# Split token rows of an input projection begin at four places modulo 256 bytes, and eight idle matmuls stand at the beginning in place of fourteen

## The chip, the cores and the metric

The kernel runs on one core of a Trainium2 chip. The metric is the device time of one execution in microseconds, lower is better. Engines are named as in the profile: PE is TensorE (PEld its weight loads), DVE is VectorE, ACT is ScalarE, POOL is GpSimd, SP is SyncE, which issues most of the DMAs.

## The reference

One layer of a hybrid decoder for 4096 prompt tokens and 64 sample tokens (8 sequences of 8), model width 1024. In short:

```python
h = _rmsnorm(x, g_pre)
z = h @ w_in                      # 1024 -> 2816 columns
cb, cc, ch, cg, q, k, v, ag, mq, mg = _split_cols(z)
u = cc * ch                       # gated short convolution
out_a = silu(cg) * cb * conv3(u)
out_b = silu(ag) * window_attention(q, k, v, sink)   # window of 128
out_c = silu(mg) * memory_attention(mq, mk, mv)      # 256 memory tokens
y = concatenate([out_a, out_b, out_c]) @ w_out
x = x + _rmsnorm(y, g_post)
```

All arrays are float32.

## The kernel before, in words

The work falls into two parts. The first, up to about 930 us, is the input projection `h @ w_in`. The second is attention and the output projection. The change touches the first alone.

**Tiles of the projection.** The 4160 tokens are cut into 8 blocks of 520 (`NBLK`), and each block into two halves of 260 (`HW`). The 22 column tiles of `w_in` are worked off in three phases (`PHASES`) as pairs, called quads `q` in the loops: four in the first two phases, three in the last. For each block and pair the product of a 2x2 matrix of weights with a 2x2 matrix of tokens is formed by seven products (`PRODUCTS`, a Strassen-Winograd scheme: A and S are weights or sums of them, B and T are tokens or sums of them). The first two blocks of the first phase are the exception: they take eight plain products (`plain_block`).

**Split numbers.** Each operand is split in two float32r parts, `hi` (the rounded copy, by ACT) and `lo` (the rest, by DVE), so that three matmuls make one product of full accuracy: w_hi x hi, w_hi x lo, w_lo x hi. `product` (L363, its matmul at L368) does this for 4 slices `k` of the contraction, 12 matmuls a call, each of 128 weights by 260 columns and each with a weight load of its own. The moving operand is a row of 260 numbers of a split token tile, the stationary operand a slice of a weight tile `w`.

**Where the operands lie.** Split token tiles come from the pool `hp`, two buffers for tag `hi` and two for `lo`. They are written in `split` (L355) for the seven-product blocks and in `x_split` (L577) for the plain ones. A tile holds 4 rows of `XR` = 320 numbers (1280 bytes, five times 256), of which the first 260 are used. The pool's address in a partition is a multiple of 256, and so are the tiles' sizes; therefore each of the rows begins at 0 modulo 256 bytes. The weight tiles of quads 0, 1 and 2 come from the pool `wa`, whose slices all begin at 0 modulo 256; those of quad 3 come from the pool `wb`, at the other end of the memory, whose slices begin at 224 modulo 256. In the profile a weight tile is named w_0, w_1, w_2 or w_3 by its quad, with a letter A or S; token tiles are named hi_3T, lo_3T and so on.

**The attention's operands**, which the prediction compares with: the scores of the window (L1248) take queries `q` as weights and keys `kst` as moving rows of 256 numbers. Odd chunks of 256 tokens hold both in the pool `pre`, where they begin at 160 modulo 256; even chunks from the second on hold them in `bq` and `keys`, where they begin at 0. The output projection (L1494) has moving rows of 512 numbers at 0 and weights at 0.

**Order.** The first phase's order on all engines is written out by hand (`manual_schedule`, L692). Ahead of the first product, PE runs matmuls on a tile `warm` of ones whose result nobody reads (L700 to L704); they need nothing but a memset of POOL. Meanwhile ACT and DVE split the first weights (`w_split`, L181) and tokens (`x_split`) as their DMAs land.

Of the kernel before, what the change touches and what calls it, by code (L numbers as in the profile page):

```python
# [9 lines left out]
F32R = mybir.dt.float32r  # L10
# [5 lines left out]
P = 128  # L16
D = 1024
KT = D // P
KH = KT // 2
# [4 lines left out]
HW = 260  # L24
XR = 320
# [22 lines left out]
def f(ap):  # L48
    return ap.bitcast(F32)
# [3 lines left out]
def hybrid_layer(ctx: ExitStack, tc: tile.TileContext, a: dict):  # L53
# [39 lines left out]
    hp = pa.enter_context(tc.tile_pool(name="hp", bufs=2))  # L93
# [68 lines left out]
    def store(dst, src):  # L162
        if store_queue[0] is G:
            G.dma_start(dst, src)
        else:
            late.append(lambda: DMA.dma_start(dst, src))
# [153 lines left out]
    def gain_of(o, k):  # L320
        kk = KH * (int(o[1]) - 1) + k
        return gpre[:, kk : kk + 1]
# [16 lines left out]
    def t_sum(ph, b, o):  # L339
# [9 lines left out]
        if ph == 1:  # L349
# [2 lines left out]
                tc.keep_in_program_order(ins)  # L352
            store(hd[b][o], ops[o])

    def split(src, name):  # L355
        hi = hp.tile([P, KH, XR], F32R, tag="hi", name=f"hi{name}")[:, :, :HW]
        lo = hp.tile([P, KH, XR], F32R, tag="lo", name=f"lo{name}")[:, :, :HW]
        S.copy(hi, src)
        V.tensor_tensor(lo, src, f(hi), op=ALU.subtract)
        return hi, lo  # L360
# [157 lines left out]
    def h_split(i):  # L518
        if i < len(steps):
            ph, b, p = steps[i]  # L520
            o = PRODUCTS[p][1]
            hs[i] = split(xs[ph, b][o], f"{ph}_{b}{o}")
# [52 lines left out]
    raw0, zz, pending, h0, kept = {}, {}, {}, {}, {}  # L575

    def x_split(b, o, meanwhile=lambda: None):  # L577
        x = xs[0, b][o]
        h0[b, o] = hi, lo = [hp.tile([P, KH, XR], F32R, tag=n, name=f"{n}0_{b}{o}")[:, :, :HW] for n in ("hi", "lo")]
        for k in range(KH):  # L580
            if k == 1:
                meanwhile()
            g = gain_of(o, k)
            S.mul(hi[:, k], x[:, k], g)
            V.scalar_tensor_tensor(lo[:, k], x[:, k], g, f(hi[:, k]), op0=ALU.mult, op1=ALU.subtract)
# [37 lines left out]
    def plain_jobs(b, s):  # L623

        gains = lambda b, *os: [lambda o=o: x_gain(0, b, o) for o in os]
        scales = lambda b, *os: [lambda o=o: x_scale(0, b, o) for o in os]
        parts = lambda b, o: [lambda: x_split(b, o)]
        fill = lambda o: [lambda q=q: first_fill(o, q) for q in range(4)]
        sums = lambda q, k: [lambda: first_sums(q, k)]
# [70 lines left out]
    idle = accumulator(1, 2, "idle")  # L700
    warm = hp.tile([P, KH, XR], F32R, tag="lo", name="warm").rearrange("p k n -> p (k n)")
    G.memset(f(warm[:, : P + 512]), 1.0)
    for n in (416, 416, 416, 416, 512, 512, 512, 416, 416, 416, 260, 260, 260, 260):
        TE.matmul(idle[:, 0, :n], warm[:, :P], warm[:, P : P + n], start=True, stop=True)  # L704
    x_split(0, "B11", lambda: first_fill("A21", 0))
    for q in range(4):
        if q > 0:
# [743 lines left out]
    class Block:  # L1451
# [10 lines left out]
        def split(self):  # L1462
# [13 lines left out]
            self.hl = [hi, lo]  # L1476

        def run(self, last, start, split, starts):
            b, m = self.b, self.m
            yn = work([P, D], "yn", f"yn{b}")  # L1480
# [4 lines left out]
            for p, (c0, c1) in enumerate(parts):  # L1485
                if p == 1:
                    split()
                acc = psum("z", f"y{b}_{p}")[:, : c1 - c0]
                j, passes = 0, 3 if m == P else 2
                for k in range(KT):  # L1490
                    if k in starts:
                        start()
                    for l, r in ((0, 0), (1, 0), (0, 1)) if m == P else ((0, 0), (0, 1)):
                        TE.matmul(acc, self.hl[l][:, k], wo[k][c0 // 512][:, r, c0 % 512 : c0 % 512 + c1 - c0], start=j == 0, stop=j == passes * KT - 1)  # L1494
                        j += 1
                if m < P:
                    S.copy(yn[:m, c0:c1], acc[m : 2 * m])
                    V.tensor_tensor(acc[:m], acc[:m], yn[:m, c0:c1], op=ALU.add)
                end = last and p == 2
                if not end:  # L1500
                    V.tensor_tensor(yn[:m, c0:c1], acc[:m], gpost[:m, c0:c1], op=ALU.mult)  # L1501
                S.activation((psum("t", "sq") if end else acc)[:m, : c1 - c0], acc[:m], AF.Square, scale=float(D) ** -0.5, accum_out=st[:m, p : p + 1])  # L1502
                if last and p == 1:
                    V.tensor_tensor(st[:m, 0:1], st[:m, 0:1], st[:m, 1:2], op=ALU.add)
# [180 lines left out]
```

## Time and profile before

| what | value |
|---|---|
| median of 3 runs | 1533.97 us (1533.04 to 1534.76) |
| profiled execution, its own time | 1536.78 us |
| its span, first to last instruction | 1535.0 us |
| PE busy | 1522.3 us, 99% of the span |
| DVE, ACT, POOL busy | 1145.1, 806.1, 379.7 us |
| mean granted TensorE clock | 0.999 |
| L368 (`product`): first and last start | 6.8 and about 930 us |

How to read it: the span counts from the first instruction. A row of the timeline has the start in us, the length in us, the engine, the line, the operation and its tiles (out<-in), the shape and the number of instructions merged. Consecutive matmuls overlap in it, because each one's length goes from its start to the end of its passage through the array; the rate at which PE works is the distance between starts. In the list of waits a row has who waited, for whom, the total in us, how many times and the longest.

### The profile page before, as it was taken

How to read it: one execution, taken by the hardware profiler on the slowest of the kernel's cores; microseconds unless marked ns; L12 is line 12 of the kernel's file. 1: busy time of each engine (PE TensorE's matmuls, PEld its weight loads, DVE VectorE, ACT ScalarE, POOL GpSimd, SP SyncE). 2: the span in 40 equal slices, each digit the busy share in tenths (PEclk: the TensorE clock that was granted, in tenths of full speed). 3: DMA queues.
4: the chain of work that ended last, by engine and by line, in shares of the span. 5: the costliest groups of instructions: out<-in, count | busy, mean ns of one | idle time of the engine just before them, and what ended most of it. 6: DMA issues, size and time to landing. Idle time of an engine off the chain costs nothing.

```text
span 1535.0 us, 30162 instructions
## 1 busy us (share of the span) xinstructions
PE 1522.3 (99%) x11337; PEld 1400.1 (91%) x11337; DVE 1145.1 (75%) x2055; ACT 806.1 (53%) x2039; POOL 379.7 (25%) x604
## 2 busy tenths in 40 slices
PE   9999999999999999999999999999999999999998
PEld 9999999999999999999999998788888888888777
DVE  6779888899887777897787678766666666666743
ACT  6776566476222222354454447755666556565632
POOL 0223332221300000000101203544444444444310
PEclk9999999999999999999999999999999999999999
DMA  9989999778755333678877788976776676776332
GB/s 263 194 223 242 267 288 269 280 239 286 193 181 180 126 126 126 217 227 284 237 262 230 228 298 257 237 151 160 148 148 148 151 162 149 160 159 148 130 110 96
DMA packets 177942, 306.28 MB, mean 200 GB/s; under 512 B 33925, under 2 KB 107653, under 8 KB 177765
## 3 DMA queue, kind: packets, MB, share of 16 engines
q1 hardware_dynamic: 130901, 227.38, 47.9%
q0 software_dynamic: 46176, 75.92, 24.1%
q8 instruction: 90, 1.47, 0.4%
q10 hardware_dynamic: 720, 1.05, 0.2%
q14 instruction: 55, 0.45, 0.1%
HBM read 197.23 MB, written 108.05 MB: 199 GB/s over the span
## 4 chain that ended last, share of the span: by engine, by line
PE 92%; DVE 4%; ACT 1%; DMA 1%; issue 1%; POOL 0%; SPq 0%; ACTq 0%; DVEq 0%; POOLq 0%
PE c L368 53%; PE y L1494 23%; PE ws L1248 4%; PE wo L1090 2%; PE wt L1271 2%; PE xs L1184 2%; PE xt L1199 2%; PE wo L1220 2%; PE wo L1226 1%; PE mem_acc L791 1%; DMA ws20A<-in_w_in 0%; DMA wr_1A<-in_w_in 0%; DMA ws18A<-in_w_in 0%; DVE x_2T L348 0%; DVE z L375 0%
## 5 line engine op out<-in xcount | busy, mean ns | idle before, releaser
L1494 PE MATMUL y<-wo,mh 128*128 128x512 f32 (+1 forms) x1040 | 350.5, 400 | 0.0
L375 DVE TENSOR_TENSOR z<-c,z 128x520 f32<-128x520 f32 (+1 forms) x308 | 194.2, 644 | 86.6 <-PE c L368 85.2
L1494 PEld LDWEIGHTS y<-wo,mh 128*128 128x128 f32 x1040 | 194.3, 188 | 39.2 <-issue 2.4
L1494 PE MATMUL y<-wo,ml 128*128 128x512 f32 (+1 forms) x520 | 201.8, 388 | 0.0
L1261 ACT ACTIVATE sm<-sm,wnm 128x128 f32<-128x128 f32 x256 | 99.6, 391 | 60.3 <-DVE wnm L1255 59.5
L1193 POOL TENSOR_SCALAR xp<-xp,xrd 128x256 f32<-128x256 f32 x128 | 74.6, 589 | 207.9 <-DVE xrd L1189 207.9
L1494 PEld LDWEIGHTS y<-wo,ml 128*128 128x128 f32 x520 | 98.2, 189 | 16.4
L1185 DVE TENSOR_REDUCE xmx<-xs 128x2 f32<-128x512 f32 x64 | 44.0, 688 | 60.0 <-PE xs L1184 59.9
L1273 ACT COPY wpt<-wt 128x512 f32<-128x512 f32 x64 | 37.2, 582 | 88.5 <-PE wt L1271 85.9
L1248 PEld LDWEIGHTS ws<-kst,q 128*128 128x128 f32 x512 | 69.7, 189 | 5.6 <-ACT xp L1188 0.7
L1501 DVE TENSOR_TENSOR yn<-y,gpost 128x512 f32<-128x512 f32 (+1 forms) x66 | 45.0, 681 | 39.9 <-PE y L1494 39.6
L1248 PE MATMUL ws<-kst,q 128*128 128x256 f32 x512 | 73.0, 283 | 0.4 <-ACT xp L1188 0.4
L1502 ACT ACTIVATE y<-y 128x512 f32<-128x512 f32 (+1 forms) x66 | 38.6, 585 | 64.0 <-DVE yn L1501 64.0
L739 POOL CAST wmask<-negs 128x256 uint8<-128x256 f32 x1 | 0.9, 877 | 267.9 <-DMA negs<-in_wmask 267.9
L1281 POOL TENSOR_SCALAR_AFFINE_SELECT wpt<-wpt 128x512 f32<-128x512 f32 x64 | 52.6, 822 | 42.2 <-ACT wpt L1273 39.3
L1188 ACT ACTIVATE xp<-xs,xnm 128x256 f32<-128x256 f32 x128 | 58.9, 464 | 7.1 <-DVE xnm L1186 7.1
L1123 POOL DMA_DIRECT2D q<-qd x64 | 42.8, 673 | 70.4 <-DMA qd<-zh 60.5
L1112 POOL DMA_DIRECT2D kst<-qd x64 | 38.6, 617 | 63.8 <-PE xt L1199 41.6
L1512 DVE SCALAR_TENSOR_TENSOR xr<-yn,yst,xr 128x1024 f32<-128x1024 f32 (+2 forms) x34 | 43.1, 1269 | 15.1 <-POOL yst L1508 13.2
L1251 DVE COPY_PREDICATED sm<-wmask,ws 128x256 f32<-128x256 uint8 x124 | 52.1, 436 | 2.4 <-ACT sm L1250 2.0
L1278 POOL TENSOR_SCALAR_AFFINE_SELECT wpv<-wpt 128x512 f32<-128x512 f32 x62 | 41.1, 662 | 50.8 <-ACT wpt L1273 50.8
L276 ACT ACTIVATE nat<-nat 104x1024 f32<-104x1024 f32 x40 | 42.2, 1056 | 19.2 <-DMA nat<-in_x_p 19.2
(962 smaller groups left out, 5096.8 us busy)
## 6 DMA issues: line engine op xcount, KB each, us to landing
q<-qd POOLq DMA_DIRECT2D x64, 384.0 KB
xr<-in_x_p SPq DMA_DIRECT2D x32, 512.0 KB
nat<-in_x_p SPq DMA_DIRECT2D x39, 416.0 KB
o_yp<-xr SPq DMA_DIRECT2D x31, 512.0 KB
md<-th POOLq DMA_DIRECT2D x48, 260.0 KB
qd<-zh SPq DMA_DIRECT2D x48, 260.0 KB
qd<-z SPq DMA_DIRECT2D x48, 260.0 KB
kst<-qd POOLq DMA_DIRECT2D x60, 192.0 KB
```

The source lines that it names most:

```text
L368: TE.matmul(bank[:, :HW], l, r, start=first and i == 0, stop=last and i == 3 * KH - 1)
L375: add = lambda dst, other: V.tensor_tensor(dst, c, other, op=ALU.add)
L1185: V.tensor_reduce(mx[:, :nb], s, axis=AX.X, op=ALU.max)
L1188: S.activation(p[:, i, :], s[:, i, :], AF.Exp, bias=nm[:, i : i + 1], scale=SCALE, accum_out=den[:, i : i + 1])
L1193: G.tensor_scalar(p[:, i, :], p[:, i, :], rd[:, i : i + 1], 0.5, op0=ALU.mult, op1=ALU.mult)
L1248: TE.matmul(s3[:, hh, :], self.q[:, 4 + 2 * (2 * half + hh) + kvh, i * P : i * P + P], self.kst[:, 2 * kvh + part, i * P : i * P + 2 * P], ...
L1251: V.copy_predicated(sm[:, 2 * half : 2 * half + 2, :], third["wmask"], third["negs"] if first else s3[:, :, 0:P])
L1261: S.activation(sm[:, hh, :], sm[:, hh, :], AF.Exp, bias=nm[:, hh : hh + 1], scale=SCALE, accum_out=den[:, hh : hh + 1])
L1281: G.affine_select(p3, p3, pattern=[[0, 4], [1, P]], compare_op=ALU.is_ge, fill=0.0, base=0, channel_multiplier=-1)
L1494: TE.matmul(acc, self.hl[l][:, k], wo[k][c0 // 512][:, r, c0 % 512 : c0 % 512 + c1 - c0], start=j == 0, stop=j == passes * KT - 1)
L1501: V.tensor_tensor(yn[:m, c0:c1], acc[:m], gpost[:m, c0:c1], op=ALU.mult)
L1512: V.scalar_tensor_tensor(self.xr[:m, cs], yn[:m, cs], st[:m, 3:4], self.xr[:m, cs], op0=ALU.mult, op1=ALU.add)
```

## The change

A helper `split_tile` hands out the split tiles in both places. It uses the same tiles of 4 x 320 numbers, but a row's 260 numbers now begin at number 8 or 16 of the 320 for `hi`, and at 40 or 48 for `lo`, in turn from one tile to the next. In bytes modulo 256 that is 32 or 64 for `hi` and 160 or 192 for `lo`. Since each tag has two buffers that are used in turn as well, each buffer has one place for good, and a step's `hi` and `lo` are always 32 and 160, or 64 and 192. The tile `warm` is not affected. Separately, the list of idle matmuls is cut after its eighth.

```diff
+    begins = {"hi": [8, 16], "lo": [40, 48]}
+
+    def split_tile(tag, name):
+
+        n = begins[tag][0]
+        begins[tag].reverse()
+        return hp.tile([P, KH, XR], F32R, tag=tag, name=name)[:, :, n : n + HW]
+
     def split(src, name):
-        hi = hp.tile([P, KH, XR], F32R, tag="hi", name=f"hi{name}")[:, :, :HW]
-        lo = hp.tile([P, KH, XR], F32R, tag="lo", name=f"lo{name}")[:, :, :HW]
+        hi, lo = split_tile("hi", f"hi{name}"), split_tile("lo", f"lo{name}")
         S.copy(hi, src)
         V.tensor_tensor(lo, src, f(hi), op=ALU.subtract)
...
     def x_split(b, o, meanwhile=lambda: None):
         x = xs[0, b][o]
-        h0[b, o] = hi, lo = [hp.tile([P, KH, XR], F32R, tag=n, name=f"{n}0_{b}{o}")[:, :, :HW] for n in ("hi", "lo")]
+        h0[b, o] = hi, lo = [split_tile(n, f"{n}0_{b}{o}") for n in ("hi", "lo")]
...
-    for n in (416, 416, 416, 416, 512, 512, 512, 416, 416, 416, 260, 260, 260, 260):
+    for n in (416, 416, 416, 416, 512, 512, 512, 416):
```

No instruction changes its place otherwise. The only difference in the order is at the beginning of PE, before the first product's 12 matmuls (idle and warm are the idle matmuls' accumulator and operand, c the first accumulator). Before:

```order
L704 MATMUL idle<-warm 128x416 x4
L704 MATMUL idle<-warm 128x512 x3
L704 MATMUL idle<-warm 128x416 x3
L704 MATMUL idle<-warm 128x260 x4
L368 MATMUL c_0_0_0_274<-hi_0B_236,w_0A_240 128x260
```

And with the change:

```order
L711 MATMUL idle<-warm 128x416 x4
L711 MATMUL idle<-warm 128x512 x3
L711 MATMUL idle<-warm 128x416
L375 MATMUL c_0_0_0_268<-hi_0B_230,w_0A_234 128x260
L375 MATMUL c_0_0_0_268<-lo_0B_231,w_0A_234 128x260
```

Two idle matmuls of 416 columns and four of 260 are gone; the products follow in the same order as before, with their lines seven higher.

## The prediction

> **What bounds the kernel now.** I read the page's busy table first, then the chain of work that ended last, then the waits of TensorE, and last the timeline of TensorE in single products.
>
> ```profile
> span 1535.0 us, 30162 instructions
> PE 1522.3 (99%) x11337; PEld 1400.1 (91%) x11337; DVE 1145.1 (75%) x2055; ACT 806.1 (53%) x2039; POOL 379.7 (25%) x604
> PE 92%; DVE 4%; ACT 1%; DMA 1%; issue 1%; POOL 0%; SPq 0%; ACTq 0%; DVEq 0%; POOLq 0%
> PE c L368 53%; PE y L1494 23%; PE ws L1248 4%; PE wo L1090 2%; PE wt L1271 2%; PE xs L1184 2%; PE xt L1199 2%; PE wo L1220 2%; PE wo L1226 1%; PE mem_acc L791 1%; DMA ws20A<-in_w_in 0%; DMA wr_1A<-in_w_in 0%; DMA ws18A<-in_w_in 0%; DVE x_2T L348 0%; DVE z L375 0%
> ```
>
> TensorE is busy for 99% of the span and holds 92% of the chain, and 53% of the chain is one line, L368: the matmuls of `product`, whose moving rows are the tiles that the change shifts. There is no wait worth removing in front of them:
>
> ```profile
> PE idle L704 <- POOL warm L702: 2.2, 1, 2.2
> PE wt L1271 <- DVE xrd L1189: 1.4, 1, 1.4
> PE c L368 <- DVE lo_3T L359: 0.9, 1, 0.9
> ```
>
> The largest wait of an L368 group is 0.9 us. So L368 costs what its matmuls cost back to back, and the question is how far apart their starts lie. The durations of the groups (282 ns) overlap and can't be added. The distance from one start to the next can. Here is one step, four products of 12 matmuls with the same split rows, each row being a product's first matmul (the column is the start):
>
> ```profile
> 152.41 0.28 PE L368 MATMUL c<-hi_3T,w_0S 128*128 128x260 f32 x1
> ...
> 153.83 0.28 PE L368 MATMUL c<-hi_3T,w_1S 128*128 128x260 f32 x1
> ...
> 155.25 0.28 PE L368 MATMUL c<-hi_3T,w_2S 128*128 128x260 f32 x1
> ...
> 156.68 0.28 PE L368 MATMUL c<-hi_3T,w_3S 128*128 128x260 f32 x1
> ...
> 158.12 0.28 PE L368 MATMUL c<-hi_3T,w_0S 128*128 128x260 f32 x1
> ```
>
> The products take 1.42, 1.42, 1.43 and 1.44 us, so 118.3 to 120 ns a matmul. The first three read weights that begin at 0 modulo 256; the fourth, w_3, reads weights that begin at 224 (pool `wb`). Its moving rows are the same ones. Places matter here, then, but by about 1.4 ns in 119.
>
> **The split rows.** The program has 7,488 matmuls at L368 (8 plain steps for 2 blocks, 7 products for 6 blocks, 7 for 8 blocks, all of 4 quads, and 7 for 8 blocks of 3 quads, each 12 matmuls). No instruction is added, and ScalarE and VectorE write the same shapes to other columns of the same tiles. Each nanosecond of distance is therefore 7.5 us, all of it on the path, since TensorE waits for nobody. What the new places do to the distance is not in the trace: all rows begin at 0 now. The nearest rows are the attention scores, with 256 columns, where two sets of buffers alternate. In the first group below keys and queries both begin at 160 modulo 256, in the second both at 0:
>
> ```profile
> 1007.76 1.11 PE L1248 MATMUL ws<-kst,q 128*128 128x256 f32 x8
> 1008.71 0.60 PE L1199 MATMUL xt<-ident,xp 128*128 128x128 f32 x4
> ```
>
> ```profile
> 1020.73 0.39 PE L1494 MATMUL y<-wo,ml 128*128 128x512 f32 x1
> ...
> 1021.87 1.11 PE L1248 MATMUL ws<-kst,q 128*128 128x256 f32 x8
> 1022.83 0.60 PE L1199 MATMUL xt<-ident,xp 128*128 128x128 f32 x4
> ```
>
> Eight matmuls up to the next group's start take 0.95 us at 160 and 0.96 us at 0: 118.75 against 120 ns, 1.25 ns less away from 0. The starts are rounded to 0.01 us, so this is 0 to 2.5 ns.
>
> The bounds. On the side of a loss: the fourth product's 1.44 us against a mean of 1.423 for the other three, 1.4 ns, on the 6,120 matmuls whose weights begin at 0 (all but w_3's 114 products of 12): +8.6 us. On the side of a gain: the five 512-column matmuls from 1020.73 to 1021.87 are 228 ns apart, the 256-column ones 120, so 256 more columns cost 108 ns, 0.42 ns a column, and 260 columns cost 110 ns with nothing else in them. That would take 9 ns from each and 67 us from the whole; it is the floor, not a likely value.
>
> The row on the gain's side at 160 is the nearest: `lo` now begins at 160 or 192, and all split rows leave 0. I take it: 1.25 ns x 7,488 = **-9.4 us**. The case against it is that there the weights moved along, and here they stay at 0 or 224.
>
> The Trainium skill speaks against any effect: in "TensorE: Matmul & The Clock Gate", Part 2, the rows that stream and the next weights are read through two independent ports, so that loading the one takes nothing from the other, and "SBUF — State Buffer", section Operand start alignment, states its rule for legality and timed nothing. By that the sum would be 0 us here. The trace disagrees by the 1.44 against 1.42 us above. The first page's matmul gap, 2.5 ns over the pure column time, would be 110.8 ns for 260 columns; it agrees with the floor worked out from rows.
>
> **The idle matmuls.** Six go: two of 416 columns and four of 260.
>
> ```profile
> 2.16 4.82 PE L704 MATMUL idle<-warm 128*128 128x416 f32 x14 [2.16 <-POOL warm L702]
> 6.82 0.28 PE L368 MATMUL c<-hi_0B,w_0A 128*128 128x260 f32 x1
> 6.93 0.28 PE L368 MATMUL c<-lo_0B,w_0A 128*128 128x260 f32 x1
> ...
> 8.84 0.39 PE L368 MATMUL c<-hi_0B,w_1A 128*128 128x260 f32 x1 [0.21 <-DVE w_1A L186]
> ```
>
> ```profile
> 5.01 0.60 ACT L182 CAST w_0A<-wr_0A 128x512 fp32r<-128x512 f32 x1
> 7.44 0.62 ACT L182 CAST w_1A<-wr_1A 128x512 fp32r<-128x512 f32 x1 [0.60 <-DMA wr_1A<-in_w_in]
> 8.09 0.69 DVE L186 TENSOR_TENSOR w_1A<-wr_1A,w_1A 128x512 fp32r<-128x512 f32 x1 [0.55 <-ACT w_1A L182]
> ```
>
> The fourteen stream 5,488 columns in 4.82 us, 0.88 ns a column: half the pace of the rows from 6.82 on, which are 0.11 to 0.12 us apart. Eight stream 3,616 columns and end near 2.16 + 3.2 = 5.3 us. The first product can then begin once w_0A is cast, at 5.6 us, instead of 6.8. It gains nothing: the third matmul of the second product still waits for w_1A, which VectorE hands over at 8.8 us, because its load lands at 7.4. Everything before 8.84 is slack. The cover is gone only if TensorE is still at half pace at 8.84. Full pace came 4.6 us after the first idle matmul; if those 4.6 us counted anew from 5.6, full pace would come at 10.2, and 1.4 us at half pace lose 0.7 us. I take 0, with +0.7 as the end.
>
> The Trainium skill ("TensorE: Matmul & The Clock Gate", Part 1) puts the change of pace at the end of a busy window of about 3.4 us whose phase is free; by an estimate from it, a window missed would cost about half of it, 1.7 us. The trace's 4.6 us fits a window and part of one before it.
>
> **The sum.** The profiled execution took 1536.78 us (its span 1535.0), 2.81 above the median of 1533.97. 1536.78 - 9.4 = 1527.4, and on the median's level **1524.6 us**.
>
> **The rivals.**
>
> *A, slower: what counts is the distance between rows and weights.* Then rows and weights at the same place are the good case and the change leaves it: with weights at 0, rows at 32, 64, 160, 192 are as far off as w_3's are now. The fourth product's row is the evidence for it, since only the weights' place differs there; against it, the wb tiles lie elsewhere in memory in other ways too. Price: 6,120 x 1.4 ns = 8.6 us, 1542.6 us; with a late full pace 1543. It decides as soon as a product with w_0 takes 1.44 us or more.
>
> *B, no difference.* Some of the four places save a nanosecond and some cost one, or the next matmul is held by the end of its weight load, whatever the rows do; PEld is 91% busy. Within 3 us: 1534. This is also what the skill's two ports would give.
>
> *C, much faster.* If the 9 ns above the floor are conflicts between the two reads and the new places avoid half of them, 4.5 x 7,488 = 34 us go: 1500. Against it: the rows above, with three combinations of places, all stay within 118 to 120 ns.
>
> That the rows would not move is no rival: in the program as built the 7,488 matmuls begin at 32, 64, 160 and 192.
>
> **How the numbers follow.** A change under 0.2% (3 us) can't be told from none. The forecast, a gain of 3 to 20 us, has 0.36; C, everything beyond that, 0.12; B 0.2; A 0.32. Faster 0.48, same 0.2, slower 0.32. The forecast alone lies in 1514 to 1531. The range takes in A's 1542.6 with its late pace and a rounding of 1 us, and on the other side C up to its 1500 us. Cases of both signs are in it, so it is wide. What is left out is the deeper half of C and an A worse than w_3 shows, 0.12 together.
>
> **What would show each step.** Right: the products of w_0 to w_2 near 1.41 us and w_3's no longer than 1.43; the page's L368 share falls; L1494 and the attention rows stay. A would be products of 1.44 us throughout; C products below 1.38. At the beginning the first L368 row should start near 5.7 us and the row with the wait for w_1A stay at 8.84; if that row comes later, or the products after it are 0.22 us a matmul, the trimmed idle matmuls cost time. The prediction is wrong if the distance does not change, or changes the other way, or if TensorE begins to wait for `hi` or `lo`.

## The result

| | before | changed |
|---|---|---|
| median of 5 runs, side by side | 1534.04 us (1533.04 to 1534.76) | 1540.01 us (1538.99 to 1543.66) |
| profiled execution: its own time, span | 1536.78, 1535.0 us | 1543.23, 1541.5 us |

The ratio is 1.0046, with a 95% interval from 1.0031 to 1.0061: the change makes the kernel slower by 6 us. The forecast was 1524.6 us; rival A said 1542.6.

The same lines of the changed kernel's page: span, busy times, and the chain that ended last by engine and by line. L375 is the old L368, L1501 the old L1494; all lines below `split` stand seven higher.

```profile
span 1541.5 us, 30150 instructions
PE 1529.6 (99%) x11331; PEld 1407.2 (91%) x11331; DVE 1147.0 (74%) x2055; ACT 806.8 (52%) x2039; POOL 380.8 (25%) x604
PE 93%; DVE 3%; DMA 2%; issue 1%; ACT 0%; POOL 0%; DVEq 0%; SPq 0%; POOLq 0%; ACTq 0%
```

PE's busy time grew by 7.3 us, that of its weight loads (PEld) by 7.1, the span by 6.5; the other engines moved by 2 us or less. The waits of PE (who, for whom: total us, times, longest) did not grow into anything of that size:

```profile
PE idle L711 <- POOL warm L709: 2.2, 1, 2.2
PE wt L1278 <- DVE xrd L1196: 1.7, 1, 1.7
PE c L375 <- ACT w_0A L182: 0.5, 1, 0.5
```

So the matmuls themselves stand further apart. Here are two steps of the changed kernel, eight products, from the same place as the step of before that the prediction shows (first matmul of each product; first column the start):

```profile
154.04 0.28 PE L375 MATMUL c<-hi_3T,w_0S 128*128 128x260 f32 x1
...
155.48 0.28 PE L375 MATMUL c<-hi_3T,w_1S 128*128 128x260 f32 x1
...
156.92 0.28 PE L375 MATMUL c<-hi_3T,w_2S 128*128 128x260 f32 x1
...
158.36 0.28 PE L375 MATMUL c<-hi_3T,w_3S 128*128 128x260 f32 x1
...
159.81 0.28 PE L375 MATMUL c<-hi_3T,w_0S 128*128 128x260 f32 x1
...
161.26 0.28 PE L375 MATMUL c<-hi_3T,w_1S 128*128 128x260 f32 x1
...
162.70 0.28 PE L375 MATMUL c<-hi_3T,w_2S 128*128 128x260 f32 x1
...
164.13 0.28 PE L375 MATMUL c<-hi_3T,w_3S 128*128 128x260 f32 x1
...
165.55 0.28 PE L375 MATMUL c<-hi_3T,w_0S 128*128 128x260 f32 x1
```

The first step has rows at 64 and 192: 1.44, 1.44, 1.44 and, with w_3, 1.45 us. The second has them at 32 and 160: 1.45, 1.44, 1.44 and, with w_3, 1.42 us. Before it was 1.42, 1.42, 1.43 and 1.44. Products with weights at 0 lost their 1.42 us, and w_3's lost or won by the place of the rows.

Over the whole projection, each product from the ninth on (from its first matmul to the next product's first) set against the same product of before:

| rows of hi / lo, weights at | products | change of each | together |
|---|---|---|---|
| 32 / 160, 0 | 221 | +16.8 ns | +3.7 us |
| 64 / 192, 0 | 228 | +11.7 ns | +2.7 us |
| 32 / 160, 224 | 54 | -27.8 ns | -1.5 us |
| 64 / 192, 224 | 56 | +8.1 ns | +0.5 us |
| over 1.475 us in either kernel (a wait in them) | 56 | | -1.5 us |

That is +3.8 us. The start of the projection adds 0.8 (below): the last L375 matmul starts at 934.69 us against 930.06, +4.6. The other 1.9 us of the two spans lie behind the projection, in a stretch that this execution had and the one of before had not (windows in us; the third column from the right is the granted TensorE clock):

```profile
960.00:965.70 5.70, 3.83 (x26) 3.14 (x25) 4.84 (x11) 2.73 (x8) 2.81 (x5) 1.00 1.31 273
965.70:969.10 3.40, 3.40 (x15) 3.22 (x16) 2.79 (x8) 2.21 (x10) 3.39 (x7) 0.50 1.21 272
969.10:975.00 5.90, 5.90 (x41) 3.67 (x41) 3.65 (x14) 4.59 (x20) 1.02 (x2) 1.00 1.50 291
```

For 3.4 us the clock is 0.50, by estimate 1.7 us of lost work. Two of the five runs of the changed kernel, 1543.23 and 1543.66 us, have a mean clock of 0.998 and are the slow end of its spread; the other three lie at 1538.99 to 1540.01 us.

The beginning, from the first idle matmul to the third product:

```profile
2.16 3.38 PE L711 MATMUL idle<-warm 128*128 128x416 f32 x8 [2.16 <-POOL warm L709]
6.06 0.58 PE L375 MATMUL c<-hi_0B,w_0A 128*128 128x260 f32 x1 [0.52 <-ACT w_0A L182]
6.44 0.42 PE L375 MATMUL c<-lo_0B,w_0A 128*128 128x260 f32 x1
...
9.12 0.42 PE L375 MATMUL c<-hi_0B,w_1A 128*128 128x260 f32 x1
9.34 0.42 PE L375 MATMUL c<-lo_0B,w_1A 128*128 128x260 f32 x1
...
10.84 0.28 PE L375 MATMUL c<-hi_0B,w_1A 128*128 128x260 f32 x1
10.96 0.28 PE L375 MATMUL c<-hi_0B,w_2A 128*128 128x260 f32 x1
```

The first product starts 0.8 us sooner than before (6.06 against 6.82), but its matmuls are 0.22 us apart until 9.98, where before they were 0.12 apart from the first on. The second product starts at 9.12 in place of 8.24, and the third at 10.96 in place of 10.15: 0.8 us late, and the ninth product is still as late (19.55 against 18.74).

### The profile page after: what moved, and what is told of

It reads as the page before. It is cut to its first block, busy times and chain, and to the rows that moved or that the text cites. A ratio compares the mean times of both kernels' runs of the same rounds, so it can differ in the third digit from the quotient of the medians.

```text
span 1541.5 us, 30150 instructions
## 1 busy us (share of the span) xinstructions
PE 1529.6 (99%) x11331; PEld 1407.2 (91%) x11331; DVE 1147.0 (74%) x2055; ACT 806.8 (52%) x2039; POOL 380.8 (25%) x604
## 4 chain that ended last, share of the span: by engine, by line
PE 93%; DVE 3%; DMA 2%; issue 1%; ACT 0%; POOL 0%; DVEq 0%; SPq 0%; POOLq 0%; ACTq 0%
PE c L375 55%; PE y L1501 22%; PE ws L1255 4%; PE wo L1097 2%; PE wt L1278 2%; PE xs L1191 2%; PE xt L1206 2%; PE wo L1227 2%; PE wo L1233 1%; PE mem_acc L798 1%; DMA qd<-z 1%; DVE z L382 0%; DMA wr_1A<-in_w_in 0%; DMA xr<-in_x_p 0%; DVE wo L186 0%
## 5 line engine op out<-in xcount | busy, mean ns | idle before, releaser
L1501 PE MATMUL y<-wo,mh 128*128 128x512 f32 (+1 forms) x1040 | 350.8, 400 | 0.0
L1501 PEld LDWEIGHTS y<-wo,mh 128*128 128x128 f32 x1040 | 194.5, 188 | 39.3 <-issue 2.4
L1501 PE MATMUL y<-wo,ml 128*128 128x512 f32 (+1 forms) x520 | 201.8, 388 | 0.0
L1501 PEld LDWEIGHTS y<-wo,ml 128*128 128x128 f32 x520 | 98.2, 189 | 16.5
L384 ACT COPY z<-c 128x520 f32<-128x520 f32 (+1 forms) x44 | 24.4, 554 | 52.9 <-PE c L375 50.0
```

## The experiments

Two theories stood at first. The theory of distance (rival A): the start of a moving row relative to the start of the weights, modulo 256 bytes, sets the spacing of the matmuls. Its rival: the loss comes from the shorter list of idle matmuls, or from the rows' own places whatever the weights do. Unless a diff shows otherwise, the kernels have fourteen idle matmuls. Times of products below are from start to start, means over all products of one kind shorter than 1.475 us.

**The two parts apart.** The changed kernel with the old list of idle matmuls:

```diff
-    for n in (416, 416, 416, 416, 512, 512, 512, 416):
+    for n in (416, 416, 416, 416, 512, 512, 512, 416, 416, 416, 260, 260, 260, 260):
```

> The new places with the fourteen idle matmuls kept. Theory 1 (the loss is mostly the rows' places, by their distance from the weights): the start loss of 0.8 us goes, the products of w_0 to w_2 stay at 1.436 to 1.444 us, so 1539 us, 5 us above the kernel before. Rival (the loss is mostly the late full pace, and later clock dips): 1535 us.

And the kernel before with the short list:

```diff
-    for n in (416, 416, 416, 416, 512, 512, 512, 416, 416, 416, 260, 260, 260, 260):
+    for n in (416, 416, 416, 416, 512, 512, 512, 416):
```

> The rows at 0 as before, with eight idle matmuls. Theory 1: only the start is later, by 0.8 us, so 1534.8 us, which can hardly be told from no change; products at 1.42 and 1.44 us as before; full pace first at about 10 us. Rival (idle matmuls carry the loss): 1538 to 1540 us.

The places alone: 1540.38 us, ratio 1.0043 [1.0029, 1.0057]. The idle matmuls alone: 1535.42 us, ratio 1.0007 [0.9998, 1.0016], which neither shows a loss of 0.8 us nor excludes it. The loss is nearly all the places'. The profile of the second kernel shows why its start cost next to nothing that time:

```profile
2.16 3.24 PE L704 MATMUL idle<-warm 128*128 128x416 f32 x8 [2.16 <-POOL warm L702]
5.69 0.39 PE L368 MATMUL c<-hi_0B,w_0A 128*128 128x260 f32 x1 [0.29 <-ACT w_0A L182]
5.92 0.28 PE L368 MATMUL c<-lo_0B,w_0A 128*128 128x260 f32 x1
```

Here the eight take 3.24 us and not 3.38: the trace's record of the granted clock begins with full speed at 5.10 us in this execution, before the last of them ended at 5.40, against 9.98 us in the changed kernel's. Apart from its waits the first product runs at 0.12 us a matmul. The third product starts at 10.43 us, 0.3 late.

**A map of distances.** In the changed kernel the places now rotate over eight, 32 bytes apart, from step to step, with hi and lo at the same place:

```diff
-    begins = {"hi": [8, 16], "lo": [40, 48]}
+    begins = {"hi": [0, 8, 16, 24, 32, 40, 48, 56], "lo": [0, 8, 16, 24, 32, 40, 48, 56]}
...
-        begins[tag].reverse()
+        begins[tag].append(begins[tag].pop(0))
```

> hi and lo begin at the same place, which moves by 32 bytes from one step to the next through all eight places modulo 256; fourteen idle matmuls. Each place meets weights at 0 and at 224. Theory 1 (only the distance of row and weights counts): a product with weights at 224 and rows at r takes what one with weights at 0 and rows at r+32 takes; 1.424 us at distance 0 and 1.441 at 32, so w_3 with rows at 224 takes 1.424. Theory 2 (the row's own place counts): the times go by r, the same for both weights, apart from a constant. The whole: 1534 to 1541 us.

One execution: 1542.02 us. This is the step before, the whole and the beginning of the step after the one with rows at 0 (first matmul of each product; the w_2 and w_3 rows at the top belong to rows at 224):

```profile
191.10 0.28 PE L375 MATMUL c<-hi_4B,w_2A 128*128 128x260 f32 x1
...
192.54 0.28 PE L375 MATMUL c<-hi_4B,w_3A 128*128 128x260 f32 x1
...
193.97 0.28 PE L375 MATMUL c<-hi_4T,w_0S 128*128 128x260 f32 x1
...
195.39 0.28 PE L375 MATMUL c<-hi_4T,w_1S 128*128 128x260 f32 x1
...
196.82 0.28 PE L375 MATMUL c<-hi_4T,w_2S 128*128 128x260 f32 x1
...
198.24 0.28 PE L375 MATMUL c<-hi_4T,w_3S 128*128 128x260 f32 x1
...
199.68 0.28 PE L375 MATMUL c<-hi_4T,w_0S 128*128 128x260 f32 x1
...
201.13 0.28 PE L375 MATMUL c<-hi_4T,w_1S 128*128 128x260 f32 x1
```

With rows at 224, w_2 (at 0) takes 1.44 us and w_3 (at 224) 1.43; with rows at 0, w_0 to w_2 take 1.42 to 1.43 and w_3 1.44; with rows at 32, w_0 takes 1.45. Over the kernel, distance 0 gives 1.424 us with weights at 0 and 1.425 with weights at 224, and each of the other seven distances gives 1.436 to 1.452. So distance 0 is good at either place of the weights, as the theory of distance says. Its stronger form, that the same distance always takes the same time, fails: at distance 128 the products take 1.452 us with weights at 0 and 1.438 with weights at 224, and at the other six distances the two differ by 0.5 to 6.2 ns.

Then the same with lo at 128 bytes, and at 64 bytes, behind hi:

```diff
-    begins = {"hi": [8, 16], "lo": [40, 48]}
+    begins = {"hi": [0, 8, 16, 24, 32, 40, 48, 56], "lo": [32, 40, 48, 56, 0, 8, 16, 24]}
```

> As the map with equal places, but lo begins 128 bytes from hi. Theory 1a (the distance modulo 128 counts): every product takes what the map with equal places gives for the same hi. Theory 1b (modulo 256, each matmul by its own distance): products differ between the maps, and hi at 32 with lo at 160 gives 1.441 us against weights at 0 and 1.414 against 224, as in the changed kernel. The whole: 1534 to 1541 us.

```diff
-    begins = {"hi": [8, 16], "lo": [40, 48]}
+    begins = {"hi": [0, 8, 16, 24, 32, 40, 48, 56], "lo": [16, 24, 32, 40, 48, 56, 0, 8]}
```

> The map again with lo 64 bytes from hi; fourteen idle matmuls. Theory 1 says nothing of unequal distances beyond this: where hi is at distance 0 and lo at 64, two of three matmuls stand well, so about 1.43 us; the rest 1.436 to 1.46. Rival (only hi and lo apart cost, not the weights): all products near one another. The whole 1540 to 1545 us.

One execution each: 1543.39 and 1541.07 us. That a further 128 bytes for lo would change nothing (theory 1a) failed; theory 1b holds for the pair that it named (1.441 and 1.414 us). Most pairs of distances give 1.43 to 1.46 us. Two beat even distance 0: hi at 64 and lo at 192 from the weights, 1.414 us with weights at 224 (with weights at 0, after a step at 32 and 160, 1.435), and hi at 0 and lo at 64, 1.415 us with weights at 0 and 1.416 at 224, where about 1.43 was expected. So there is something better than what the kernel before had, and lo's distance counts beside hi's.

Last, finer steps of 16 bytes with hi and lo alike:

```diff
-    begins = {"hi": [8, 16], "lo": [40, 48]}
+    begins = {"hi": [0, 4, 8, ..., 60], "lo": [0, 4, 8, ..., 60]}
```

> The map with hi and lo at the same place in steps of 16 bytes, sixteen places; fourteen idle matmuls. Theory 1: distance 0 alone gives 1.424 us, against weights at 0 and at 224 alike; 16 and 240 bytes off already cost 1.436 or more. If the good place is broad, 16 and 240 give 1.42 to 1.43. The whole 1541 to 1543 us.

One execution, 1539.14 us. That only distance 0 would do failed: with weights at 0, distances 16, 80, 144 and 240 give 1.420 to 1.425 us too, 48 gives 1.430, distance 112 the longest, 1.460, and the rest (176, 208 and every multiple of 32 but 0) 1.439 to 1.452. With weights at 224 some of these differ: 16 gives 1.434 and 80 gives 1.438. No simple rule in the distance fits this list.

**Distance 0 everywhere.** The tile `gpre` lies in front of the weights' pool. Half as large, it moves the weights of quads 0 to 2 and the rows by 32 bytes, from 0 to 224, where w_3's are already. The base is the kernel before:

```diff
-    gpre = const.tile([P, 2 * KT], F32, name="gpre")[:, :KT]
+    gpre = const.tile([P, KT], F32, name="gpre")
```

> The kernel before, with 32 bytes less ahead of the weights' first pool, so that the weights of quads 0 to 2 and all split rows begin at 224 modulo 256, where the weights of quad 3 begin already; fourteen idle matmuls. Every row then stands at distance 0 from its weights. Theory 1 (distance): all products 1.424 us; those of w_3 lose 17 ns each, 112 of them 1.9 us, so 1532.4 us. Theory 2 (a place of its own is good or bad): w_0 to w_2 change from 1.424 us and the whole moves by several us.

1533.92 us, ratio 0.9998 [0.9987, 1.0008]. In its profile the last L368 matmul starts 2.7 us earlier (927.32 against 930.06), but over the runs no difference can be told. Its products take 1.422 to 1.427 us for the most part (454 of 568 shorter than 1.475 us), but 67 take 1.440, and 27 of these follow one another:

```profile
437.51 0.28 PE L368 MATMUL c<-hi_2T,w_0S 128*128 128x260 f32 x1
...
439.33 0.28 PE L368 MATMUL c<-hi_2T,w_1S 128*128 128x260 f32 x1
...
440.77 0.28 PE L368 MATMUL c<-hi_2T,w_2S 128*128 128x260 f32 x1
...
478.21 0.28 PE L368 MATMUL c<-hi_3T,w_0S 128*128 128x260 f32 x1
...
479.76 0.28 PE L368 MATMUL c<-hi_3T,w_1S 128*128 128x260 f32 x1
...
481.19 0.28 PE L368 MATMUL c<-hi_3T,w_2S 128*128 128x260 f32 x1
```

The product from 437.51 has a wait of 0.3 us for `lo` in it (1.82 us). From 439.33 to 478.21 all 27 products take 1.440 us, then one takes 1.55, and from there on they take 1.42 again. All these rows and weights begin at 224. The places, then, do not fix the time alone: the same ones can run at two paces, and PE can change from one to the other where it waits.

**The good pair made constant.** On that base (all weights at 224) and with the helper `split_tile`, one place for all steps: hi 64 and lo 192 bytes from the weights.

```diff
+    begins = {"hi": [16], "lo": [48]}
```

> As the kernel with all operands at 224, but every hi row 64 and every lo row 192 bytes from its weights, the combination that w_3 has with half of the tiles in the changed kernel (1.414 us a product) and that w_0 to w_2 have with the other half (1.414 to 1.444). If 1.414 is what this distance gives when nothing else disturbs it: 624 products x 10 ns less than 1.424, so 1526 to 1528 us. If a product keeps the rhythm in which it began: most stay at 1.436 to 1.444, so 1539 to 1542 us.

1527.67 us, ratio 0.9946 [0.9932, 0.996]: faster than both kernels. The products, through a change of step:

```profile
155.59 0.28 PE L375 MATMUL c<-hi_3T,w_3S 128*128 128x260 f32 x1
...
157.00 0.28 PE L375 MATMUL c<-hi_3T,w_0S 128*128 128x260 f32 x1
...
158.41 0.28 PE L375 MATMUL c<-hi_3T,w_1S 128*128 128x260 f32 x1
```

Each takes 1.41 us; of 566 products shorter than 1.475 us, 540 take 1.413 or 1.414, and 16 take 1.440 or 1.441, in pairs right behind a product that waited. Its control is the same kernel with every row 32 bytes earlier, at 32 and 160 from the weights:

```diff
-    begins = {"hi": [16], "lo": [48]}
+    begins = {"hi": [8], "lo": [40]}
```

> All weights begin at 224, hi at distance 32 and lo at distance 160 from them in every step; against the kernel with distances 64 and 192 every row only begins 32 bytes earlier. If the distance sets the time: 1.44 us a product and about 1540 to 1542 us, as the changed kernel. If the distance does not matter and the constant places made the kernel at 64/192 fast: 1.414 us and about 1528 us.

1542.93 us, ratio 1.0051 [1.0036, 1.0066]: slower than the kernel before, by about as much as the changed kernel. Nearly all its products (552 of 567) take 1.44 us, and none less than 1.439, though it waits as often:

```profile
151.94 0.28 PE L375 MATMUL c<-hi_3B,w_3A 128*128 128x260 f32 x1
...
153.38 0.28 PE L375 MATMUL c<-hi_3T,w_0S 128*128 128x260 f32 x1
...
154.82 0.28 PE L375 MATMUL c<-hi_3T,w_1S 128*128 128x260 f32 x1
```

Between these two kernels nothing differs but 32 bytes in the start of the rows, and 15 us. They were timed apart, but the kernel before, timed beside each, differed by 0.9 us only (1535.05 and 1534.20), and in the two profiles the last L375 matmul starts at 922.17 and 935.38 us, so the difference arises in the projection. And the second good pair, hi at 0 and lo at 64:

```diff
-    begins = {"hi": [16], "lo": [48]}
+    begins = {"hi": [0], "lo": [16]}
```

> All weights begin at 224, hi at distance 0 from them and lo at distance 64, in every step, fourteen idle matmuls. If the pair of distances of hi and lo sets the time: products of 1.413 us as the pair 0/64 showed where eight places rotated, and about 1528 us in all. If what was seen there came from the rotation (the step before), about 1.424 to 1.44 us and 1534 to 1541 us.

1527.97 us, ratio 0.9958 [0.9943, 0.9973], products of 1.413 us: the pair is good outside the rotation too.

**Why 64 / 192 did not help the changed kernel.** It has rows at 64 and 192 with weights at 0 in every second step, a good pair by the above, yet these products take 1.436 us in the mean: 193 of 229 take 1.435 to 1.444, 28 take 1.413 to 1.416, 24 of the latter in the last phase, where PE often waits. The changed kernel with that pair in all steps (weights as they were):

```diff
-    begins = {"hi": [8, 16], "lo": [40, 48]}
+    begins = {"hi": [16], "lo": [48]}
```

> The changed kernel with one pair of places for all steps, 64 for hi and 192 for lo, in place of two pairs in turn; weights as there, at 0 for w_0 to w_2 and 224 for w_3; fourteen idle matmuls. If the changed kernel's products at 64/192 are 1.436 us because each step comes after one at 32/160: w_0 to w_2 at 1.414 us, w_3 near 1.45, about 1531 us. If it is the weights' place 0 as against 224 that spoils them: 1.436 to 1.44 us and about 1540 us.

1530.85 us, ratio 0.9978 [0.9968, 0.9988].

```profile
152.93 0.28 PE L375 MATMUL c<-hi_3T,w_1S 128*128 128x260 f32 x1
...
154.34 0.28 PE L375 MATMUL c<-hi_3T,w_2S 128*128 128x260 f32 x1
...
155.75 0.28 PE L375 MATMUL c<-hi_3T,w_3S 128*128 128x260 f32 x1
...
157.20 0.28 PE L375 MATMUL c<-hi_3T,w_0S 128*128 128x260 f32 x1
...
158.61 0.28 PE L375 MATMUL c<-hi_3T,w_1S 128*128 128x260 f32 x1
```

With weights at 0 the pair gives 1.414 us now; only w_3's, 96 and 224 bytes from its weights, is longer, 1.443 us in the mean. So it was the alternation that spoiled the pair, not the weights' place. How a step at 32 and 160 reaches into the next step is open. That it leaves the next step at the slower of two paces would fit the products at one place that took 1.440 us above, but w_3's products take 1.414 us in the middle of products of 1.44, so it is not simply that a slow product makes the next one slow.

**Eight idle matmuls on the fast kernel.**

```diff
-    for n in (416, 416, 416, 416, 512, 512, 512, 416, 416, 416, 260, 260, 260, 260):
+    for n in (416, 416, 416, 416, 512, 512, 512, 416):
```

> The kernel with distances 64 and 192 from weights at 224, now with eight idle matmuls. If the number of idle matmuls only shifts the phase in which full pace comes: within 1 us of the same kernel with fourteen, 1527 to 1529 us. If eight lose what the changed kernel's profile lost at the beginning every time: 0.8 us more.

1529.65 us, ratio 0.9968 [0.9956, 0.9981], 2.0 us above the kernel with fourteen. The two were timed apart and their intervals touch (0.9956 to 0.996), so a cost of the short list is likely here and not shown. Its profile shows the changed kernel's start again, and longer:

```profile
2.16 3.38 PE L711 MATMUL idle<-warm 128*128 128x416 f32 x8 [2.16 <-POOL warm L709]
6.41 0.58 PE L375 MATMUL c<-hi_0B,w_0A 128*128 128x260 f32 x1 [0.87 <-ACT w_0A L182]
...
11.20 0.58 PE L375 MATMUL c<-hi_0B,w_1A 128*128 128x260 f32 x2
11.62 0.28 PE L375 MATMUL c<-lo_0B,w_1A 128*128 128x260 f32 x1
...
11.87 0.28 PE L375 MATMUL c<-hi_0B,w_2A 128*128 128x260 f32 x1
```

Nearly all of the first two products run at 0.22 us a matmul, and the third starts at 11.87. In the eleven profiles with fourteen idle matmuls it starts between 9.87 and 10.81, and at most six of the first thirty distances are near 0.22 us; with eight it starts at 10.43, 10.96 and 11.87, with five, thirteen and nineteen of them.

## Why the prediction was wrong

**What bounds the kernel: right.** The time is the spacing of L368's matmuls. Without any new wait, a shift of the rows by 32 bytes moved the whole kernel by up to 15 us (1527.67 against 1542.93), in the mean 2.0 ns for each of 7,488 matmuls.

**The split rows: wrong in sign, and this is the step that failed.** The prediction took -1.25 ns a matmul from the attention scores (0.95 us for eight at 160, 0.96 at 0) as "the nearest" row, because the new places too were away from 0. It named the flaw itself: "there the weights moved along". In those rows keys and queries begin at the same place in both groups, distance 0 both times, so they could say nothing of a distance, and the difference shown was within the rounding of the starts (over all such groups of the trace, in whole ns, it is about 0.4 ns a matmul). What the change varies is the distance, and with weights at 0 it cost 1.4 ns a matmul at 32 and 160 (16.8 ns in 12) and 1.0 at 64 and 192 (11.7 ns), where a gain of 1.25 was forecast. The row that did vary the distance was the fourth product's, and it was used as a bound. That its 1.4 ns hit the size is in part luck: its rows stand at 32 for `hi` and `lo` alike, a pair that the changed kernel does not have.

**Rival A: right that the rows' start against the weights' counts, and nearly right in size,** with a chance of 0.32 where 0.48 went to a gain. Its premise that equal starts are the good case and all others cost alike is wrong: 64 and 192, or 0 and 64, are better than equal starts where they are constant, and the 2.7 us at 64 and 192 come from the alternation, which A does not have. So the nearness of its sum is partly luck. Its 8.6 us compare with the 3.7 + 2.7 = 6.4 us of products with weights at 0. It left out w_3's products, which it had no reason to hold fixed: their distances change too, and half of them become 1.414 us (-1.5 and +0.5 us). The products with a wait in them gave another 1.5 back.

**Rival B and the two ports: ruled out.** The Trainium skill's rule ("TensorE: Matmul & The Clock Gate", Part 2), that the streaming rows and the next weights are read through independent ports, would make the places cost nothing; the runs disagree by those 15 us for 32 bytes. By what means the two starts act on the spacing, the runs do not show.

**Rival C: its premise was half right.** Some of the spacing does depend on the places and can be taken back, but the best that was found is 117.8 ns a matmul (1.414 us for 12), not the 114 that C needed, and the changed kernel, which alternates, has it in a small part of its products only.

**The idle matmuls: taken at 0, measured 0.8 us in the profiled execution.** The mechanism given for the loss, half pace still on when the second product comes, is what happened; its end value of 0.7 us was near. The cover that the prediction named, the wait for w_1A up to 8.84 us, was indeed gone: at half pace the second product starts at 9.12, and nothing waits for w_1A any more. The moment of full pace differs between executions of the short list (5.10, 9.98 and 11.60 us in three profiles), and with it the delay of the third product (0.3, 0.8 and 1.7 us against the 10.15 of the kernel before). Over the runs of the kernel before, a loss of this size can be neither shown nor excluded (1.0007 [0.9998, 1.0016]).

## What to carry to other kernels

Where one kind of matmul fills the time, read its spacing from start to start, and see whether it differs between operands that lie at different places modulo 256 bytes; if so, try the moving rows' starts against the weights' as a pair, for every operand in the rhythm, and hold the pair constant (here 1.413 to 1.46 us for the same 12 matmuls). Look for stretches of another pace at the same places before a mean is put down to the places. A row that is to price a change must vary the thing that the change varies: a comparison in which both operands move together does not price the distance between them. Idle matmuls that are cut at the beginning need a check that the pace has changed before the first real one; the start of the third product shows it.

## What the runs showed of the hardware

- Twelve float32r matmuls of 128 x 128 x 260 take 1.413 to 1.46 us by the starts of the rows relative to the weights modulo 256 bytes. Equal starts, the case of the kernel before, are good (1.424 us) but not the best (1.413 us at 64 and 192, or 0 and 64). Distances that are multiples of 32 need not behave like those of 16: with weights at 0, 144 gave 1.421 us, 128 and 160 gave 1.452 and 1.441. With weights at 224, 128 gave 1.438, and 160 gave 1.442 in the map of eight places and 1.432 in that of sixteen, so the distance of a step's own rows is not the whole rule.
- The same places can run at two paces: with all operands at 224, 27 products in a row took 1.440 us between two products that waited, and 1.422 to 1.427 before and after.
- In the first microseconds the matmuls are 0.22 us apart, later 0.12, and the change falls on the first record that the trace has of the granted clock, 1.00 from 9.98 us on in the changed kernel's profile. The window from 5.00 to 9.90 us reads 1.00 as well, because the trace records nothing there.
- The moment at which full pace comes is not fixed by the first matmul, which is at 2.16 us each time: by that record it is 5.10, 9.98 and 11.60 us with eight idle matmuls, and 5.11 to 8.05 us in the eleven profiles with fourteen. Between the changes of the clock that a trace records lie whole multiples of 3.413 us, in all fourteen traces (1525.758 us is 447 of them, 955.732 is 280).
- A granted clock of 0.50 for 3.4 us stood right behind PE's wait of 1.7 us at L1278 in the profile of the changed kernel. Whether the wait brought it about was not tried.
